# Scores taken ahead in the expert layer: where plain fp32 products stand, and which engine splits the weights for the others

## The chip, the core and the metric

The kernel runs on one core of one Trainium2 chip. The metric is device time in microseconds (us). A core has TensorE (PE in the profile, its weight loads PEld), VectorE (DVE), ScalarE (ACT), GpSimd (POOL), and SyncE (SP), which here only issues transfers. Each engine works through its own list of instructions in a fixed order and waits where an operand isn't ready.

## The reference

Two layers of a diffusion backbone over 512 latent and 256 context tokens of width 1024. Each layer ends in an expert layer (PEER) with 16384 experts, each one row of `exp_u` and one of `exp_v`. A token picks 16 experts for each of 8 heads:

```python
def retrieve(xc):                                     # 128 tokens
    q = (xc @ w_q).reshape(128, 8, 2, 128)
    s = jnp.einsum('thpd,hpnd->thpn', q, sub_keys)    # against 2 x 128 keys a head
    sv, si = lax.top_k(s, 16)
    ...                                               # 16 best sums of pairs
    top_s, top_j = lax.top_k(cand_s, 16)
    e_idx = jnp.take_along_axis(cand_i, top_j, axis=-1)
    gate = jax.nn.softmax(top_s, axis=-1)
    act = gelu(jnp.einsum('thkd,td->thk', exp_u[e_idx], xc))
    return jnp.einsum('thk,thkd->td', gate * act, exp_v[e_idx])
```

## The kernel before

The expert layer (`ffn`, line 1509 on) treats most token tiles of 128 densely: four in layer 0, three in layer 1 (`nd`, so 512 or 384 columns, `ND`). For these it computes the scores of all 16384 experts, as 128 blocks of 128 experts, multiplies them by a sparse matrix of gates, and multiplies the result into `exp_v`. The other tiles (two of the context in layer 0, one in layer 1) gather their rows of the table by indirect transfers on GpSimd.

A score block is made by `score` (line 1538) in one of two forms.

- Plain fp32 (`native`, through `linear`, line 661): one transfer of 512 KB puts the block's weights straight into the tile `wh`, and TensorE multiplies eight slices of them with the fp32 tokens `h[2]`. These stand in tiles that the program calls `row`. The profile shows 16 matmul records per block, `mm<-row,wh`.
- Split (`split`, line 647, and `product`, line 672): the transfer goes to a tile `w`. ScalarE rounds it to `wh` (line 657), a second engine subtracts to get the low part `wl` (line 658), and TensorE makes 24 products with the high and low parts of the tokens, `hhi` and `hlo`: `mm<-hlo,wh`, `mm<-hhi,wh`, and last `mm<-hhi,wl`.

The pool `wts` holds two pairs of `wh` and `wl` in layer 0 and three in layer 1. The tile `w` has three buffers in layer 0 (pool `wload`) and two in layer 1.

After the retrieval (`retrieve`), a stage runs once per layer that is called the spreading stage here. For each tile, `candidates` (line 1441 on) finds the 16 experts of each head, on VectorE with some additions on GpSimd (`ci`, line 1457). For each dense tile `d`, `spread` (line 1746) then builds the gate matrix in 16 rounds, four to each quarter `q`. A round has four comparisons and products on VectorE (`A`, `B`, `H`, `L`, lines 1770 to 1773), 32 small fp16 products on TensorE (`ch<-A,H` and `ch<-A,L`), and two evacuations on ScalarE (`stage`, line 1781). Each quarter ends in a store of 2048 KB (`Wd<-stage`, line 1783). A tile's rounds begin with transposes on TensorE (line 1756) that need VectorE's `af` (line 1753).

The spreading gives TensorE little to do, so 44 of the 128 score blocks (`SK`, the list `early`) are computed inside this stage, ahead of their use, and parked in memory (`gd`). `ahead(n)` (line 1547) brings their number up to `n`, and after each quarter it is asked for a share of the 44 in proportion. In layer 0 all 44 blocks are plain fp32. In layer 1 the even ones are plain and the odd ones split, with GpSimd as the second engine. The other 84 blocks are split with VectorE in the main loop behind the stage. A scheduler fixes the order on each engine from the program; the rounds and the blocks are interleaved there.

Of the kernel before, what the change touches and what calls it, by code (L numbers as in the profile page):

```python
# [156 lines left out]
SK = 44  # L157
# [87 lines left out]
class K:  # L245
# [1263 lines left out]
    def ffn(self, li):  # L1509
# [4 lines left out]
        nc, io = self.nc, self.io  # L1514
        nd = 3 if li else 4
# [6 lines left out]
        gd = self.dram.tile([SK, 128, ND], F32, name=f"gd{li}")  # L1522
        with ExitStack() as es:
# [14 lines left out]
            def score(a, eng, native=False):  # L1538
                if native:
                    p = self.linear(io["uT"][li, a], (None, None, h[2]), ND)  # L1540
                else:
                    p = self.product(self.split(io["uT"][li, a], eng), h, ND)
                g = dp.tile([128, ND], F32, name="g", bufs=4 if li else 3)
                nc.scalar.activation(g, p[:, 0:ND], AF.Gelu)  # L1544
                return g

            def ahead(n):
                while nsk[0] < min(n, SK):
                    nc.sync.dma_start(gd[nsk[0]], score(early[nsk[0]], nc.gpsimd, not li or nsk[0] % 2 == 0))  # L1549
                    nsk[0] += 1  # L1550

            nsk, early = [0], [(2 * n + 1) * 64 // SK for n in range(SK)]
            with ExitStack() as e1:
                tk = P("topk", e=e1)
                sv = tk.tile([128, nt, 16, 16], F32, name="sv")
                si = tk.tile([128, nt, 16, 16], U32, name="si")
                with ExitStack() as e2:
                    hs = []
                    hc = None if li else P("hc", e=e2)
                    for b in ((1,) if li else (1, 0)):  # L1560
                        T = TL if b else TC
                        hb = self.norm_apply(li, 1, b, self.xs if b else self.xc, T, self.rl if b else self.rc, fp if b else hc)
                        if b:
                            h = hb
                        for j, i in enumerate(gathered if b == li else ()):
                            xk = pk.tile([128, 1024], F32, name="xt", tag=("xk", "acc")[j])
                            self.token_major(hb[2], i, xk)
                            nc.sync.dma_start(xd[j], xk)
                        hs.append((hb, T, 2 if b > li else 0))
                    for _ in self.retrieve(li, hs, sv, si, self.wts):  # L1570
                        yield 10
                t2, st = P("cand", 2, e=e1), P("wst", 2, e=e1)
                due = 0.0
                for n, i in enumerate(gathered + dense):
                    self.candidates(sv[:, i], si[:, i], idx[i], gate[i], tk, t2)
                    yield 5
                    if i in gathered:
                        if li:
                            picks.fetch(2)
                        continue  # L1580
                    d = n - len(gathered)
                    for q in self.spread(d, idx[i], gate[i], Wd, tk, st):
                        if q is not None:
                            ahead((SK * (4 * d + q) + 4 * nd - 1) // (4 * nd))
                        elif not li:
                            due += GP
                            picks.fetch(int(due))
                        yield 3
                ahead(SK)
            base, NP = len(picks.rows), picks.n - (0 if li else REST)  # L1590
            cp, ew = P("coef", 2), ExitStack()
            wv = P("wv", 3 if li else 4, e=ew)
# [212 lines left out]
```

## Time and profile before

| what | value |
|---|---|
| three runs | 5423.01, 5433.58 (median), 5465.13 us |
| the profiled execution | 5431.71 us, of it 5429.9 us span |
| granted TensorE clock over the span | 0.932 |
| TensorE, VectorE, ScalarE, GpSimd busy | 91%, 70%, 35%, 22% |
| spreading stage of layer 0, with the blocks ahead | about 1430 to 1850 us |
| spreading stage of layer 1, with the blocks ahead | about 4210 to 4530 us |

Times inside the profile count from the start of the span. A busy share over the whole span mixes many stages, so the two spreading stages are read alone, in windows: which engine is full there, and what the other one waits for. The start of one matmul record to the start of the next tells its price better than its length, since matmuls overlap.

### The profile page before, as it was taken

The page shows a single profiled execution, that of the slowest core. Times are in us where ns is not written, and L with a number is a line of the kernel's source. Part 1 is how long each engine was busy: PE and PEld are TensorE (multiplying, and loading weights), DVE is VectorE, ACT ScalarE, POOL GpSimd, SP SyncE. Part 2 cuts the span into 40 slices and gives each one's busy share as a digit, 9 for nine tenths or more (in the row PEclk, how much of TensorE's full clock was granted, in tenths as well). Part 3 has the DMA queues.
Part 4 walks back from the last instruction along what each step waited for, and adds up shares of the span by engine and source line. Part 5 has one row for each costly group of instructions (what it writes and reads, how often), then busy time and mean ns, then how long its engine had stood idle before and what let it go on. Part 6 is the DMA issues. An engine that isn't in the chain of part 4 may idle for free. (4 is left out here: it accounts for less than half of the span.)

```text
span 5429.9 us, 75527 instructions
## 1 busy us (share of the span) xinstructions
PE 4933.1 (91%) x28525; PEld 3699.6 (68%) x28525; DVE 3819.7 (70%) x8269; ACT 1895.7 (35%) x3396; POOL 1185.2 (22%) x891
## 2 busy tenths in 40 slices
PE   7987999889989999999999779888889889999998
PEld 4765676547644588887878436656657667888887
DVE  6367666656896488888888874666636986777776
ACT  5322222443254333333333212222223454444442
POOL 2322122221200022222222241211122321111110
PEclk9987899899999999999999899777889999999999
DMA  6310121342365788888888773100022668888885
GB/s 203 105 37 20 58 87 48 114 156 66 110 188 162 238 328 317 321 330 320 320 328 318 289 271 112 66 1 1 1 76 84 198 197 300 324 321 310 321 321 206
DMA packets 392490, 1028.15 MB, mean 189 GB/s; under 512 B 31443, under 2 KB 198644, under 8 KB 336572
## 3 DMA queue, kind: packets, MB, share of 16 engines
q1 hardware_dynamic: 336828, 620.64, 34.1%
q0 software_dynamic: 55296, 402.68, 19.7%
q8 instruction: 224, 3.67, 0.3%
q14 instruction: 142, 1.16, 0.1%
HBM read 920.19 MB, written 103.02 MB: 188 GB/s over the span
## 5 line engine op out<-in xcount | busy, mean ns | idle before, releaser
L203 POOL DMA_INDIRECT row<-in_uv,idx x384 | 538.4, 1402 | 1884.4 <-DVE acc L241 1606.7
L657 ACT ACTIVATE wh<-w 128x1024 fp32r<-128x1024 f32 x515 | 545.5, 1060 | 977.9 <-PE mm L272 444.5
L272 PE MATMUL mm<-hlo,wh 128*128 128x512 f32 (+2 forms) x2240 | 804.5, 364 | 17.6 <-DVE hlo L636 6.7
L272 PE MATMUL mm<-hhi,wh 128*128 128x512 f32 (+2 forms) x2240 | 796.6, 360 | 0.0
L658 DVE TENSOR_TENSOR wl<-w,wh 128x1024 fp32r<-128x1024 f32 x424 | 516.0, 1219 | 252.7 <-ACT wh L657 242.2
L241 DVE SCALAR_TENSOR_TENSOR acc<-row,act,acc 128x1024 f32<-128x1024 f32 x381 | 490.3, 1287 | 34.0 <-ACT act L237 33.6
L272 PE MATMUL mm<-hhi,wl 128*128 128x512 f32 (+2 forms) x2240 | 481.5, 356 | 0.0
L219 DVE SCALAR_TENSOR_TENSOR row<-row,xk 128x1024 f32<-128x1024 f32 x384 | 470.6, 1226 | 14.2 <-DMA row<-in_uv,idx 13.9
L272 PEld LDWEIGHTS mm<-hlo,wh 128*128 128x128 f32 x2240 | 427.8, 191 | 77.3 <-DVE hlo L636 9.0
L272 PE MATMUL mm<-row,wh 128*128 128x512 f32 (+1 forms) x1056 | 453.3, 572 | 29.0 <-DMA wh<-in_uT 24.4
L272 PEld LDWEIGHTS mm<-hhi,wh 128*128 128x128 f32 x2240 | 427.9, 191 | 53.0 <-issue 1.4
L272 PEld LDWEIGHTS mm<-hhi,wl 128*128 128x128 f32 x2240 | 392.9, 189 | 44.6 <-issue 1.2
L658 POOL TENSOR_TENSOR wl<-w,wh 128x1024 fp32r<-128x1024 f32 x91 | 227.2, 2500 | 616.9 <-ACT wh L657 368.1
L272 PEld LDWEIGHTS mm<-row,wh 128*128 128x128 f32 x1056 | 194.4, 194 | 208.3 <-issue 159.3
L236 ACT ACTIVATE act<-act 128x1 f32<-128x1 f32 x384 | 76.0, 198 | 523.1 <-DVE row L219 522.9
L1781 ACT ACTIVATE stage<-ch 128x512 f32<-128x512 f32 x224 | 218.2, 1103 | 61.4 <-PE ch L272 59.5
L1544 ACT ACTIVATE g<-mm 128x512 f32<-128x512 f32 (+1 forms) x256 | 137.8, 539 | 230.6 <-PE mm L272 200.1
L272 PE MATMUL rw<-wh,cl 128*128 128x512 f32 x512 | 200.8, 392 | 7.4 <-DVE cl L1612 4.4
L272 PE MATMUL mm<-h,wh 128*128 128x512 f32 (+1 forms) x480 | 194.2, 551 | 11.9 <-DMA hv<-in_hvec 10.7
L272 PE MATMUL rw<-wl,ch 128*128 128x512 f32 x512 | 200.5, 392 | 0.0
L272 PE MATMUL ch<-wh,cl 128*128 128x512 f32 x512 | 199.7, 390 | 0.0
L272 PE MATMUL ch<-wl,ch 128*128 128x512 f32 x512 | 199.4, 390 | 0.0
(541 smaller groups left out, 10390.3 us busy)
## 6 DMA issues: line engine op xcount, KB each, us to landing
w<-in_uv SPq DMA_DIRECT2D x256, 512.0 KB
w<-in_uT SPq DMA_DIRECT2D x190, 512.0 KB
Wd<-stage SPq DMA_DIRECT2D x28, 2048.0 KB
w<-in_mod_w SPq DMA_DIRECT2D x192, 256.0 KB
wh<-in_uT SPq DMA_DIRECT2D x66, 512.0 KB
W<-Wd SPq DMA_DIRECT2D x32, 1024.0 KB
W<-Wd SPq DMA_DIRECT2D x32, 768.0 KB
w<-in_wq SPq DMA_DIRECT2D x32, 512.0 KB
```

The lines of the kernel that those rows point to most:

```text
L203: self.nc.gpsimd.indirect_dma_start(out=row, out_offset=None, in_=self.k.io[f"uv{self.li}"], in_offset=bass.IndirectOffsetOnAxis(ap=self.t ...
L219: nc.vector.scalar_tensor_tensor(row[:, 0:1024], row[:, 0:1024], 1.0, self.x, op0=OP.mult, op1=OP.mult, accum_out=act)
L236: nc.scalar.activation(act, act, AF.Gelu)
L241: nc.vector.scalar_tensor_tensor(self.acc, row[:, 1024:], act, self.acc, op0=OP.mult, op1=OP.add)
L272: self.nc.tensor.matmul(out, lhsT, rhs, start=start, stop=stop, skip_group_check=True)
L657: self.nc.scalar.activation(wh[:, s], w, AF.Copy)
L658: eng.tensor_tensor(wl[:, s], w, wh[:, s].bitcast(F32), op=OP.subtract)
L1544: nc.scalar.activation(g, p[:, 0:ND], AF.Gelu)
L1781: nc.scalar.activation(stage[:, :, u:u + 4].rearrange("p a t -> p t a"), p, AF.Copy, scale=1 / GS)
```

## The change

The plain products move to the front of each stage and the split ones to the back, and VectorE replaces GpSimd in the split. As long as the tile being spread belongs to the first half (`2 * d < nd`), a block is plain fp32; after that it is split, with VectorE as the second engine.

```diff
-            def ahead(n):
+            def ahead(n, native):
                 while nsk[0] < min(n, SK):
-                    nc.sync.dma_start(gd[nsk[0]], score(early[nsk[0]], nc.gpsimd, not li or nsk[0] % 2 == 0))
+                    nc.sync.dma_start(gd[nsk[0]], score(early[nsk[0]], nc.vector, native))
                     nsk[0] += 1
...
-                            ahead((SK * (4 * d + q) + 4 * nd - 1) // (4 * nd))
+                            ahead((SK * (4 * d + q) + 4 * nd - 1) // (4 * nd), 2 * d < nd)
...
-                ahead(SK)
+                ahead(SK, False)
```

With `nd` = 4, the last call for a tile of the first half is at d = 1, q = 3 and asks for ceil(44 x 7 / 16) = 20 blocks. Layer 0 so has 20 plain and 24 split blocks in place of 44 and 0. With `nd` = 3, tiles 0 and 1 count as the first half, the last call there asks for ceil(44 x 7 / 12) = 26, and layer 1 has 26 plain and 18 split blocks in place of 22 and 22.

On TensorE, in layer 0, the first split block stands just ahead of the transposes of the third tile (d = 2). The piece of the difference begins behind the last round of the second tile:

```order
 L272 LDWEIGHTS L
 L272 MATMUL ch<-A,L 128x128
-L272 MATMUL mm<-row,wh 128x512 x15
+L272 MATMUL mm<-row,wh 128x512 x9
+L272 MATMUL mm<-hlo_11440,wh 128x512
+L272 MATMUL mm<-hhi_11439,wh 128x512
+L272 MATMUL mm<-hlo_11440,wh 128x512
+L272 MATMUL mm<-hhi_11439,wh 128x512
```

Nine products of plain blocks are left where fifteen were (in this order a plain block counts eight), and two whole split blocks and the start of a third follow them ahead of the transposes.

On VectorE, in the rounds of layer 0's last tile (d = 3), nothing but the rounds stood before:

```order
L1773 TENSOR_TENSOR L<-B,T_15770 128x1024
L1770 TENSOR_TENSOR A<-iota_92,T_15770 128x1024
L1771 TENSOR_TENSOR B<-iota_92,T_15770 128x1024 x2
L1772 TENSOR_TENSOR H<-B,T_15770 128x1024
L1773 TENSOR_TENSOR L<-B,T_15770 128x1024
L1771 TENSOR_TENSOR B<-iota_92,T_15770 128x1024
L1772 TENSOR_TENSOR H<-B,T_15770 128x1024
```

Now the same place in the changed kernel:

```order
L1773 TENSOR_TENSOR L<-B,T_15990 128x1024
L658 TENSOR_TENSOR wl<-w,wh 128x1024
L1770 TENSOR_TENSOR A<-iota_92,T_15990 128x1024
L1771 TENSOR_TENSOR B<-iota_92,T_15990 128x1024
L658 TENSOR_TENSOR wl<-w,wh 128x1024
L1772 TENSOR_TENSOR H<-B,T_15990 128x1024
L1773 TENSOR_TENSOR L<-B,T_15990 128x1024
```

The 24 subtractions of layer 0 stand like this between comparisons and products of rounds: four ahead of the first round of d = 2, nine between there and the end of the candidates of d = 3, and eleven in or behind the rounds of d = 3. In layer 1 two stand ahead of the rounds of d = 2 and sixteen in or behind them.

On GpSimd, in the candidates of layer 1, the subtractions stood among the gathers of rows (`row<-in_uv,idx`):

```order
L658 TENSOR_TENSOR wl<-w,wh 128x1024
L203 DMA row<-in_uv,idx_33528 128x2048 x2
L658 TENSOR_TENSOR wl<-w,wh 128x1024
L203 DMA row<-in_uv,idx_33528 128x2048 x2
L658 TENSOR_TENSOR wl<-w,wh 128x1024
```

In the changed kernel only the gathers and the additions of the candidates are left there:

```order
L1457 TENSOR_TENSOR ci<-sf 128x8x6
L1457 TENSOR_TENSOR ci<-sf 128x8x8
L203 DMA row<-in_uv,idx_34008 128x2048 x5
L1457 TENSOR_TENSOR ci<-sf 128x8x16
L1457 TENSOR_TENSOR ci<-sf 128x8x8
```

Outside the two stages the order of the instructions is the same in both kernels.

## Rows read from the trace of the kernel before

**Rows 1.** The page, part 1: busy time, share of the span, instructions.
```profile
PE 4933.1 (91%) x28525; PEld 3699.6 (68%) x28525; DVE 3819.7 (70%) x8269; ACT 1895.7 (35%) x3396; POOL 1185.2 (22%) x891
```

**Rows 2.** Windows, layer 0: length; PE, PEld, DVE, ACT, POOL busy; clock, DMA share, GB/s.
```profile
1580.00:1630.00 50.00, 42.26 (x300) 24.66 (x298) 48.24 (x112) 33.54 (x37) 0.00 (x0) 0.98 0.77 223
1633.00:1850.00 217.00, 199.89 (x898) 100.59 (x897) 105.66 (x232) 80.64 (x98) 5.06 (x8) 1.00 0.59 176
```

**Rows 3.** Windows, layer 1, same columns.
```profile
4210.00:4420.00 210.00, 177.00 (x1066) 133.69 (x1064) 201.36 (x553) 103.36 (x130) 61.29 (x47) 0.93 0.64 199
4420.00:4490.00 70.00, 62.53 (x423) 47.17 (x424) 47.09 (x66) 37.88 (x46) 17.42 (x5) 0.98 0.61 187
```

**Rows 4.** Waits of TensorE, 1640 to 1850 us: total, times, longest.
```profile
PE mm L272 <- DMA wh<-in_uT: 11.6, 8, 2.1
PE ch L272 <- ACT stage L1781: 5.0, 16, 0.7
```

**Rows 5.** Waits of TensorE, 4210 to 4540 us.
```profile
PE tr L1756 <- DVE af L1753: 13.2, 3, 5.1
...
PE ch L272 <- DVE L L1773: 4.3, 5, 1.5
PE mm L272 <- DMA wh<-in_uT: 4.0, 2, 2.2
```

**Rows 6.** Timeline of TensorE, layer 0: start, length, instruction, wait before it.
```profile
1728.56 7.11 PE L272 MATMUL mm<-row,wh 128*128 128x512 f32 x16 [1.82 <-DMA wh<-in_uT]
1735.51 0.38 PE L1756 MATMUL tr<-ident,af 128*128 128x128 f32 x2
...
1851.23 0.80 PE L272 MATMUL mm<-hlo,wh 128*128 128x512 f32 x1
1851.86 0.39 PE L272 MATMUL mm<-hhi,wh 128*128 128x512 f32 x1
...
1857.11 0.39 PE L272 MATMUL mm<-hlo,wh 128*128 128x512 f32 x1
```

**Rows 7.** Timeline of TensorE, layer 1: a split block, then a plain one.
```profile
4401.25 0.63 PE L272 MATMUL mm<-hlo,wh 128*128 128x384 f32 x1
...
4405.73 5.32 PE L272 MATMUL mm<-row,wh 128*128 128x384 f32 x16
4410.59 0.63 PE L272 MATMUL mm<-hlo,wh 128*128 128x384 f32 x1
```

**Rows 8.** Groups by form, 4230 to 4560 us: the subtraction on VectorE, on GpSimd.
```profile
L658 DVE TENSOR_TENSOR wl<-w,wh 128x1024 fp32r<-128x1024 f32 x11 | 13.1, 1217 | 11.0 <-ACT wh L657 7.3 <-PE mm L272 3.6
...
L658 POOL TENSOR_TENSOR wl<-w,wh 128x1024 fp32r<-128x1024 f32 x19 | 54.2, 2850 | 183.9 <-ACT wh L657 173.1 <-PE ch L272 10.8
```

**Rows 9.** Waits of VectorE, 1640 to 1850 us.
```profile
DVE H L1772 <- PE ch L272: 52.2, 7, 17.1
DVE A L1770 <- ACT T L1760: 23.6, 1, 23.6
```

**Rows 10.** Timeline of GpSimd and VectorE, layer 1: instructions alone and beside a subtraction.
```profile
4404.66 2.79 POOL L658 TENSOR_TENSOR wl<-w,wh 128x1024 fp32r<-128x1024 f32 x1 [18.50 <-ACT wh L657]
...
4224.22 0.99 DVE L1474 TENSOR_TENSOR e<-e 128x1600 int16<-128x1600 int16 x1
4405.26 3.03 DVE L1474 TENSOR_TENSOR e<-e 128x1600 int16<-128x1600 int16 x1
...
4234.37 2.43 DVE L1457 TENSOR_TENSOR cs<-sv 128x128 f32<-128x128 f32 x1
4414.33 3.04 DVE L1474 TENSOR_TENSOR e<-e 128x1600 int16<-128x1600 int16 x1
```

**Rows 11.** Timeline of SyncE's queue: the issue behind the store of 1791.37 us.
```profile
1791.37 0.52 SPq L1783 DMA_DIRECT2D Wd<-stage  x1
1795.23 2.16 SPq L1549 DMA_DIRECT2D gd<-g  x1
```

**Rows 12.** The costliest groups of the page: the rounding on ScalarE.
```profile
L657 ACT ACTIVATE wh<-w 128x1024 fp32r<-128x1024 f32 x515 | 545.5, 1060 | 977.9 <-PE mm L272 444.5
```

## The prediction

> **What bounds the kernel now.** I read the page first, then windows over the two spreading stages, then the waits of TensorE and VectorE in them, then single blocks on the timeline. The page's first part says that TensorE is busy 91% of the span [rows 1], so a stage is shortened by taking work or waiting off TensorE, unless another engine is full there.
>
> In layer 0, from the third tile on, TensorE is that engine: it is busy 199.89 of 217 us, VectorE 105.66. Just before, up to 1630 us, VectorE is the fuller one with 48.24 of 50 us against 42.26 [rows 2]. VectorE's largest waits there are for TensorE's small products (52.2 us) and for evacuated transposes that TensorE makes late (23.6 us) [rows 9]. TensorE's own largest wait is for the weights of plain blocks, 11.6 us in 8 times [rows 4].
>
> In layer 1 it is the other way round until 4420 us: VectorE is busy 201.36 of 210 us, TensorE 177.00 [rows 3]. TensorE waits 13.2 us for `af` in front of the transposes, and 4.3 us for `L` [rows 5]. From 4420 us on TensorE leads again, with 62.53 of 70 us against 47.09 [rows 3].
>
> **The change part by part, layer 0.** Here 24 plain blocks become split ones, all from the end of the second tile on, where TensorE leads.
>
> TensorE's work: a plain block of 512 columns takes 1735.51 - 1728.56 = 6.95 us. A split block in a steady run takes 23 steps in 1857.11 - 1851.86 = 5.25 us, so 5.25 x 24 / 23 = 5.48 us for 24; with the first record after a change of kind it is 1857.11 - 1851.23 = 5.88 us [rows 6]. The split blocks will be cut up by rounds and pay some of that entry again and again. I take 5.6, nearer the steady value: 24 x (6.95 - 5.6) = 32.4 us less, with 25.7 and 35.3 as ends.
>
> The Trainium skill ("FP8 and Floating Point Precision", section "TensorE Precision Notes") says that true fp32 takes four passes through the array. Three split products against four passes would make a split block 6.95 x 3 / 4 = 5.21 us and the saving 24 x 1.74 = 41.8 us. The steady run of the trace is slower than that, 5.48 us, so the rows decide and the page's figure stays outside my ends.
>
> The waits for weights: a plain block's transfer goes straight into `wh`, of which there are two, so it can't be issued before TensorE has finished two blocks back; behind a 2048 KB store the queue itself is late by another 2.16 us for the next issue [rows 11]. A split block's transfer goes into one of three `w`, which are free as soon as ScalarE and the subtraction have read them. So of the 11.6 us [rows 4] I expect 7 to go, with ends 0 (the queue stays late, and the wait is for `wh` from ScalarE instead) and 11.6.
>
> ScalarE gets 24 roundings of 1.06 us [rows 12], 25.4 us. It is busy 80.64 of 217 us there [rows 2], so they lie beside its idle time. Behind a rounding that waits stand evacuations of the rounds, for which TensorE waits 5.0 us already [rows 4]; that is part of the loss in order below.
>
> VectorE gets 24 subtractions of 1.217 us [rows 8]. Four stand ahead of the first round of the third tile, where VectorE has been the fuller engine [rows 2], so they may push that tile's rounds back by 4 x 1.22 = 4.9 us (ends 0 and 4.9); I count all of it. The other 20 (24.4 us) have 52.2 + 23.6 = 75.8 us of waits to lie in [rows 9]. But they stand between the instructions of rounds, and one that waits for ScalarE or for a free `wl` holds the `H` and `L` behind it, and with them TensorE's small products. With that cover all gone they would cost 24.4 us. I take 5 us.
>
> Sum for layer 0: -32.4 - 7 + 4.9 + 5 = -29.5 us, from -46.9 to +3.6 with all ends on one side.
>
> **Layer 1.** TensorE: a split block of 384 columns takes 4405.73 - 4401.25 = 4.48 us, a plain one 4410.59 - 4405.73 = 4.86 us [rows 7]. Four more blocks are plain: 4 x 0.38 = 1.5 us more.
>
> GpSimd loses 22 subtractions of 2.85 us each [rows 8]. It isn't the bound, but beside one of them a VectorE instruction stands still: the same step took 0.99 us alone and 3.03 us when GpSimd's ran from 4404.66 us [rows 10]. I find twelve such stretched instructions from 4234 to 4415 us, of which rows 10 show the first and the last. At 2.04 us each that is 24.5 us of VectorE's 201.36. What it is worth on the path is capped by what TensorE waits for VectorE: 13.2 + 4.3 = 17.5 us [rows 5]. TensorE also has about 13 more plain blocks in place of split ones before 4420 us, 13 x 0.38 = 5 us, which fills part of these gaps. 17.5 - 5 leaves 12.5; I take 12 us, ends 0 and 17.5.
>
> The Trainium skill ("SBUF — State Buffer", section "Who interferes with whom") says that a VectorE instruction with two SBUF inputs and a GpSimd instruction that reads SBUF shut each other out for a whole instruction. By that a hold could last GpSimd's whole 2.79 us, 33.5 us for twelve; the trace's pair shows 2.04, and the cap is the same. It speaks against the change in one place: the new subtractions have two inputs as well, and can be held by GpSimd's additions for the candidates.
>
> The plain blocks of the back half had 4.0 us of waits for weights [rows 5]: 2 of them go, ends 0 and 4. Two subtractions stand ahead of the third tile's rounds: 2.4 us, ends 0 and 2.4. The other sixteen, 19.5 us, have 70 - 47.09 = 22.9 us of VectorE's idle time [rows 3]: 2 us, ends 0 and 19.5.
>
> Sum for layer 1: 1.5 - 12 - 2 + 2.4 + 2 = -8.1 us, from 1.5 - 17.5 - 4.0 = -20.0 to 1.5 + 2.4 + 19.5 = +23.4.
>
> Both together: -29.5 - 8.1 = -37.6 us on 5431.7 us, the profiled execution, so 5394.1. The median of the three runs is 1.9 us above the profiled one, so I predict 5396 us. What is late next: in layer 0 from the third tile on still TensorE, with VectorE 24 us closer to it; in layer 1 until 4420 us both at once.
>
> **The rivals.** (A) *Everything falls in.* Queues stay in step: TensorE gets the steady 35.3 and all 11.6 us in layer 0, the whole 17.5 and 4.0 us in layer 1, and only the subtractions that stand ahead of rounds and the 1.5 us are paid: -35.3 - 11.6 + 4.9 = -42.0 and 1.5 - 17.5 - 4.0 + 2.4 = -17.6. That gives 5434 - 59.6 = 5374 us. For it speaks that VectorE has three times the idle time that it needs in layer 0 [rows 9]; against it that TensorE would have to run both stages almost without a gap.
>
> (B) *VectorE becomes the bound.* All 42 subtractions end on the path, 42 x 1.217 = 51.1 us, and TensorE's saving is worth nothing, since it now waits for rounds; only the 24.5 us of holds by GpSimd come back. The time is 5434 + 26.6 = 5460 us, slower than before. The place is the rounds of the third and fourth tile. It decides once VectorE's rounds with subtractions take longer than TensorE's rounds with blocks. From 1633 to 1850 us VectorE is busy 105.7 us, with 24 subtractions 135; TensorE's 199.9 us [rows 2] less 32.4 are 167.5. VectorE would have to lose more than 32 us to order. That speaks against it.
>
> (C) *The transfers decide.* SyncE's queue serves stores, scores and weights in one order and is late behind each 2048 KB store [rows 11]; if the weights for split blocks come no earlier than now, TensorE's saving turns into waits, for `w` and `wh` instead of `wh` alone. Layer 0 gains nothing, layer 1 keeps its 8 us: 5425 us. For it speaks that DMA is what TensorE waits for most in layer 0 [rows 4]; against it that the DMA share there is only 0.59 [rows 2] and that the bytes stay the same.
>
> **How the numbers follow.** My forecast gets 0.58, A 0.24, B 0.05, C 0.13. The range goes from 5365 us, below A (with both layers at their lowest ends, -46.9 and -20.0, it would be 5367), to 5430 us, just above C; B lies outside. One per cent, 54 us, is about what a measurement of this kernel can tell from no change. A lies 60 us below the median, beyond it; the lower edge of my own forecast adds 0.03, so faster by over 1% has 0.27. B is within 1% (+0.5%), and only a worse B goes beyond: 0.02. The rest, 0.71, is within 1%.
>
> **What would show it right or wrong.** In the changed kernel's profile: split blocks of layer 0's back half at 5.5 to 5.9 us each where no round cuts in; TensorE's wait for weights after the third tile's start at a few us; the spreading stage of layer 0 with its early blocks some 30 us shorter, that of layer 1 some 8; no VectorE instruction of 3 us in layer 1 where its neighbours take 1. It is wrong if TensorE's waits for `H`, `L` or `stage` grow by more than 10 us in the third and fourth tile (toward B), if it waits for `wh` or `wl` as long as it did for weights (toward C), or if a stage outside these two changes its length by more than a few us.

## The result, and the profile after

| | before | changed |
|---|---|---|
| median of 13 runs each, us | 5437.35 (5411.38 to 5465.13) | 5380.35 (5362.8 to 5401.56) |
| the profiled execution / its span, us | 5431.71 / 5429.9 | 5380.15 / 5378.2 |
| granted clock over the span | 0.932 | 0.935 |

The changed kernel is faster: the ratio is 0.9897, with a 95% interval of 0.9881 to 0.9914, or 57.0 us between the medians. The prediction was 5396 us.

The page's first part of the changed kernel, against [rows 1], tells almost nothing of this: TensorE has 38.5 us less work, and its share is 91% as before.

```profile
PE 4894.6 (91%) x28685; PEld 3719.0 (69%) x28685; DVE 3836.6 (71%) x8311; ACT 1918.1 (36%) x3416; POOL 1118.1 (21%) x869
```

More is to be seen when each stage is cut at marks that both kernels have: the transposes of the first tile (line 1756), those of the third tile, and the first product of the main loop. The stretch up to the third tile is called the *first part* below, the one behind it the *second part*. First the kernel before, in windows; the columns are those of rows 2.

```profile
1506.35:1638.03 131.68, 117.48 (x699) 64.75 (x700) 124.29 (x346) 74.76 (x87) 8.20 (x14) 0.95 0.66 194
1638.03:1866.25 228.22, 207.57 (x940) 108.05 (x938) 110.06 (x220) 87.64 (x107) 6.00 (x9) 1.00 0.61 186
4271.27:4420.36 149.09, 127.27 (x871) 96.27 (x871) 141.55 (x322) 86.70 (x103) 32.72 (x23) 0.95 0.66 197
4420.36:4537.25 116.89, 103.36 (x624) 80.58 (x624) 60.02 (x78) 55.21 (x69) 24.27 (x9) 0.99 0.73 235
```

The same four parts of the changed kernel:

```profile
1512.50:1642.14 129.64, 120.90 (x737) 70.73 (x737) 126.17 (x336) 78.35 (x91) 10.46 (x16) 0.99 0.72 213
1642.14:1831.77 189.63, 171.92 (x1092) 134.39 (x1093) 134.74 (x254) 110.25 (x126) 1.81 (x7) 1.00 0.68 211
4235.31:4367.56 132.25, 124.13 (x778) 78.92 (x779) 124.89 (x324) 78.14 (x94) 9.70 (x15) 0.99 0.75 212
4367.56:4482.59 115.03, 104.50 (x741) 98.74 (x739) 68.52 (x93) 64.99 (x81) 0.94 (x1) 0.99 0.77 251
```

Read them in pairs. Layer 0 gains 2.0 us in the first part and 38.6 in the second, 40.6 together. TensorE's busy time there falls from 117.48 + 207.57 = 325.05 to 292.82, by 32.2, and its time without work from 34.9 to 26.5, by 8.4. Layer 1 gains 16.8 and 1.9 us. There TensorE's busy time falls by 2.0 only; what shrinks is the time without work, from 35.3 to 18.6. The stretch ahead of layer 1's first part (the *opening* below, from the start of the last group of key products, `rw<-key,qT`, to the first tile's transposes) also gets shorter, from 66.2 to 60.0 us.

That makes 65.6 us at the places of the change, while the spans differ by 51.7. The difference comes from stretches where both kernels have the same instructions in the same order; the last group of layer 0's key products ahead of the stage starts at 1429.24 us before and at 1435.23 in the changed kernel, and in the runs below, which change nothing ahead of this point either, anywhere from 1422.17 to 1464.16. The prediction would have taken a few us of this kind as a sign against itself; with such a spread they are none. So the experiments are judged by the length of their parts, beside the time.

The sum of a layer says more than a single part, because the scheduler moves blocks across the marks. Counted by TensorE's records (16 of `mm<-row,wh` or 8 of `mm<-hlo,wh` a block), layer 0 before has 11.2 early blocks in the first part and 23.2 in the second, the changed kernel 12.6 and 21.9. In layer 1 the opening and the two parts have 10.4, 17.5 and 15.7 before, and 9.4, 16.2 and 18 in the changed kernel (the two blocks of the main loop that each second part ends with are left out).

Waits of TensorE in the changed kernel, layer 0's second part (engine, line waited for: total, times, longest). They answer to [rows 4]; behind them stands only one of 1.3 us for `H`.

```profile
PE ch L272 <- ACT stage L1781: 9.5, 26, 0.7
PE tr L1756 <- DVE af L1753: 2.4, 2, 1.5
PE ch L272 <- DVE A L1770: 1.9, 5, 0.5
```

The waits for weights of plain blocks are gone, and waits for `stage` have grown from 5.0 to 9.5 us. In layer 1's first part these and 0.4 us for `H` are all that is left of [rows 5]; the waits for `L` have vanished:

```profile
PE ch L272 <- ACT stage L1781: 5.8, 19, 0.7
PE tr L1756 <- DVE af L1753: 4.8, 2, 3.9
```

A split block that nothing cuts into, on the timeline of TensorE in layer 0's second part, against [rows 6]: 1801.23 - 1795.79 = 5.44 us.

```profile
1795.79 0.39 PE L272 MATMUL mm<-hlo,wh 128*128 128x512 f32 x1
...
1801.23 0.39 PE L272 MATMUL mm<-hlo,wh 128*128 128x512 f32 x1
```

### The profile page after: what moved, and what is told of

It reads as the page before. It is cut to its first block, busy times and chain, and to the rows that moved or that the text cites. A ratio compares the mean times of both kernels' runs of the same rounds, so it can differ in the third digit from the quotient of the medians.

```text
span 5378.2 us, 75892 instructions
## 1 busy us (share of the span) xinstructions
PE 4894.6 (91%) x28685; PEld 3719.0 (69%) x28685; DVE 3836.6 (71%) x8311; ACT 1918.1 (36%) x3416; POOL 1118.1 (21%) x869
## 5 line engine op out<-in xcount | busy, mean ns | idle before, releaser
L272 PE MATMUL mm<-hlo,wh 128*128 128x512 f32 (+2 forms) x2400 | 863.9, 364 | 16.4 <-DVE acc L1635 6.8
L272 PE MATMUL mm<-hhi,wh 128*128 128x512 f32 (+2 forms) x2400 | 859.9, 362 | 0.0
L658 DVE TENSOR_TENSOR wl<-w,wh 128x1024 fp32r<-128x1024 f32 x466 | 568.4, 1223 | 295.5 <-ACT wh L657 272.7
L272 PE MATMUL mm<-hhi,wl 128*128 128x512 f32 (+2 forms) x2400 | 523.6, 359 | 0.0
L272 PEld LDWEIGHTS mm<-hhi,wl 128*128 128x128 f32 x2400 | 421.9, 188 | 51.7 <-issue 1.9
L272 PE MATMUL mm<-row,wh 128*128 128x384 f32 (+1 forms) x736 | 296.6, 546 | 6.7 <-ACT g L1544 4.4
L658 POOL TENSOR_TENSOR wl<-w,wh 128x1024 fp32r<-128x1024 f32 x69 | 165.8, 2408 | 424.5 <-PE mm L272 226.0
L272 PEld LDWEIGHTS mm<-row,wh 128*128 128x128 f32 x736 | 134.0, 193 | 113.8 <-issue 67.2
L272 PE MATMUL rw<-wh,ch 128*128 128x512 f32 x512 | 200.4, 391 | 0.0
L272 PE MATMUL ch<-wh,ch 128*128 128x512 f32 x512 | 200.0, 391 | 0.0
```

Of the source, the lines that this page charges most:

```text
L272: self.nc.tensor.matmul(out, lhsT, rhs, start=start, stop=stop, skip_group_check=True)
L658: eng.tensor_tensor(wl[:, s], w, wh[:, s].bitcast(F32), op=OP.subtract)
```

## The experiments

Parts are given as first + second part. For orientation: before 131.7 + 228.2 in layer 0 and 149.1 + 116.9 in layer 1; changed 129.6 + 189.6 and 132.2 + 115.0. All ratios are to the kernel before. How far such lengths can be trusted is seen where runs share a layer's program: the sum of its two parts then lies between 319.3 and 319.9 us in layer 0 as changed (five runs), 358.4 and 359.9 as before (three), 247.1 and 249.0 in layer 1 as changed (five), and 265.1 and 267.6 as before (three).

### The two layers apart

The changed kernel with layer 1 as before:

```diff
-score(early[nsk[0]], nc.vector, native)
+score(early[nsk[0]], nc.gpsimd if li else nc.vector, nsk[0] % 2 == 0 if li else native)
```

> Layer 0 as in the changed kernel (20 plain blocks, then 24 split by VectorE), layer 1 as before (plain and split in turns, GpSimd). Theory: the two layers' gains are independent and add up. From the first transposes of the third tile to the first product of the main loop, layer 0 takes 228.2 us before and 189.6 us after the change; here 190 +-3. Layer 1 from its first tile's transposes to the main loop takes 266.0 before and 247.3 after; here 266 +-3. In all some 36 to 41 us less than before (-0.7%). Rival: the gain of layer 1 is a consequence of layer 0's (rows gathered earlier, a different clock); then layer 1 is shortened here as well and the time is close to the changed kernel's.

Measured: 5406.26 us, ratio 0.9942 (0.9918 to 0.9965). Layer 0 has 130.7 + 188.8, layer 1 148.2 + 119.4.

And the changed kernel with layer 0 as before:

```diff
-score(early[nsk[0]], nc.vector, native)
+score(early[nsk[0]], nc.vector, native if li else True)
```

> Layer 0 as before (44 plain blocks), layer 1 as in the changed kernel (26 plain, then 18 split by VectorE). Theory: layer 0's back part takes 228 +-3 us, layer 1's stage 247 +-3, in all 16 to 21 us less than before (-0.35%). Rival (layer 1's gain hangs on layer 0's): layer 1's stage stays at 266.

Measured: 5419.74 us, ratio 0.9962 (0.9944 to 0.9981); 132.0 + 227.5 and 132.8 + 116.3, with an opening of 60.7 us in layer 1. The parts of both are as expected; the first run's whole gain, 33.2 us, is a little below the 36 to 41 expected. The gains, 0.58% and 0.38%, add up to 0.96%, beside 1.03% for the whole change, so the layers can be studied one at a time.

### Layer 0: how much is the late weights?

The kernel before, where plain blocks of layer 0 put their weights into `wh` and the idle `wl` by turns, four buffers in place of two:

```diff
-                    p = self.linear(io["uT"][li, a], (None, None, h[2]), ND)
+                    p = self.ps("mm")
+                    w = self.wts.tile([128, 8, 128], F32, name="wl" if not li and nsk[0] % 2 else "wh")
+                    nc.sync.dma_start(w, io["uT"][li, a])
+                    for k in range(8):
+                        self.mm(p[:, :ND], w[:, k], h[2][k][:, :ND], k == 0, k == 7)
```

> The kernel before, all of layer 0's early blocks plain fp32, but their weights go by turns into the buffers of wh and of wl (which stand idle there), so four blocks can be under way in place of two. It takes the waits for weights alone out of the gain: TensorE waited 6.8 us for them between the first and the third tile's transposes of layer 0 and 11.6 us behind (18.4 us). Theory (most of layer 0's 40.6 us is products saved, 24 blocks at about 1.35 to 1.5 us): those waits fall under 4 us, the stage from the first transposes to the main loop takes 342 to 352 us (359.9 before, 319.3 after the change), in all 8 to 18 us less than before. Rival (the late weights were the whole cost of a plain block): it takes 320 to 328 us.

Measured: 5422.21 us, ratio 0.9964 (0.9938 to 0.9991); layer 0 has 127.8 + 211.9 = 339.6 us, a little shorter than expected. The two largest waits of TensorE from 1500 to 1850 us in this kernel (its `stage` and `af` are lines 1785 and 1757):

```profile
PE ch L272 <- ACT stage L1785: 10.9, 33, 0.7
PE tr L1760 <- DVE af L1757: 10.5, 3, 9.2
```

Four more follow, of 1.9 us and less, and no wait for weights is among them. So 20.3 of the 40.6 us can be had without splitting a single block, from weights that come in time; and in the other 20.3 us the products' 32.2 us have partly been given back.

### Layer 0: what the subtractions cost

The changed kernel without the subtraction in layer 0's 24 split blocks (the rounded part is used a third time, so TensorE's work is the same):

```diff
-            eng.tensor_tensor(wl[:, s], w, wh[:, s].bitcast(F32), op=OP.subtract)
-        return wh, wl
+            if not self.bare:
+                eng.tensor_tensor(wl[:, s], w, wh[:, s].bitcast(F32), op=OP.subtract)
+        return wh, wh if self.bare else wl
...
+                    self.bare = not li
                     nc.sync.dma_start(gd[nsk[0]], score(early[nsk[0]], nc.vector, native))
+                    self.bare = False
```

> The changed kernel, with one edit: the 24 split blocks taken ahead in layer 0 leave the subtraction out and use the rounded part a third time (the low part of these weights is left out of the result). Layer 1 as in the changed kernel (132.2 and 115.0 us). Doing each subtraction twice cost 16.6 us for 29 us of work. Theory: the first 29 us cost something too, since VectorE's spare time in the rounds is used up in places: 3 to 12 us less over both parts, of it up to 4.9 in the first. Rival: the first 24 are hidden whole and only what goes beyond the cover is paid, so 317 to 321 us for both parts, as in the changed kernel (319.3).

Measured: 5388.74 us, ratio 0.9895 (0.9844 to 0.9946); layer 0 has 127.6 + 187.4 = 315.0 us. The time can't tell this from the changed kernel; the parts are 2.0 and 2.2 us shorter, 4.2 in all. Only the sum tells what the subtractions cost, because the first part holds about half a split block less here (37 products of split blocks in place of 50). TensorE's largest wait in the second part, for `stage`, is nearly what it was: 8.1 us in 23 times.

And with each of these subtractions done twice:

```diff
-            eng.tensor_tensor(wl[:, s], w, wh[:, s].bitcast(F32), op=OP.subtract)
+            for _ in range(1 + self.twice):
+                eng.tensor_tensor(wl[:, s], w, wh[:, s].bitcast(F32), op=OP.subtract)
```

> The changed kernel, but in layer 0 each of the 24 early subtractions is done twice on VectorE (the same values again), 24 x 1.22 = 29 us more of VectorE's work in the back part. It measures the cover. Theory (the subtractions lie beside waits of VectorE): back part 190 to 197 us, 0 to 7 more than the 189.6 of the changed kernel. Rival (VectorE is the next bound and each subtraction is on the path): 205 to 219 us.

Measured: 5404.59 us, ratio 0.993 (0.9905 to 0.9954); 136.3 + 199.6 = 335.9 us, 16.6 more than the changed kernel. The second part lies between what the two theories gave for it; the first, for which they gave nothing, is 6.7 us longer and holds almost a block more (73 products of split blocks against 50). Taken with the run ahead of it: the first 24 x 1.22 = 29 us of VectorE's work cost 4.2 us, the second 29 us cost 16.6. The cover is real and nearly used up.

The same 24 blocks split by GpSimd:

```diff
-score(early[nsk[0]], nc.vector, native)
+score(early[nsk[0]], nc.vector if li else nc.gpsimd, native)
```

> The changed kernel, but layer 0's 24 split blocks are split by GpSimd. Theory: TensorE's work is that of the changed kernel, and each subtraction on GpSimd holds VectorE by some 2 us, 24 x 2 = 49 us beside about 55 us of VectorE's idle time: the back part of layer 0 takes 193 to 205 us (228.2 before, 189.6 after), the front 130 +-3. Rival (it is the products alone, the second engine doesn't matter where TensorE leads): 188 to 192 us.

Measured: 5390.73 us, ratio 0.9901 (0.9866 to 0.9937); 133.3 + 201.6 = 334.9 us, 15.6 longer than with VectorE, and the second part is where the theory expected it. Windows of its two parts, then of the kernel without the subtraction:

```profile
1516.95:1650.25 133.30, 118.09 (x724) 68.36 (x724) 129.76 (x335) 78.45 (x91) 19.31 (x19) 0.97 0.72 213
1650.25:1851.87 201.62, 177.19 (x1106) 139.95 (x1106) 130.47 (x232) 111.35 (x127) 63.59 (x28) 0.97 0.64 196
```

```profile
1522.68:1650.31 127.63, 119.16 (x724) 68.74 (x724) 123.18 (x335) 78.21 (x91) 11.00 (x16) 0.98 0.71 207
1650.31:1837.73 187.42, 173.75 (x1105) 137.60 (x1106) 111.07 (x232) 108.12 (x127) 4.12 (x7) 1.00 0.71 220
```

The third figure behind the comma is VectorE. Both kernels give it the same 567 instructions (335 + 232) and no subtraction, and yet it is busy 129.76 + 130.47 = 260.2 us in the one and 123.18 + 111.07 = 234.3 in the other. 24 subtractions on GpSimd cost VectorE 26 us; in the changed kernel, which does them itself, it is busy 126.17 + 134.74 = 260.9 us. With GpSimd as the second engine, fourteen of VectorE's instructions run 1.2 to 2.5 us past the shortest of their form, 27.1 us in all. Handing this work to GpSimd saved VectorE nothing. What makes the kernel slower is that the rounds come later: over both parts TensorE waits 12.1 us for `H` in place of 2.8, 15.4 for `af` in place of 11.7, and 2.2 for `L`, for which it waited nowhere. It has no wait for `wl` itself.

### Layer 1: the engine, the place, or both?

Order of plain and split as changed, GpSimd as the second engine again in layer 1:

```diff
-score(early[nsk[0]], nc.vector, native)
+score(early[nsk[0]], nc.gpsimd if li else nc.vector, native)
```

> The changed kernel, but layer 1's 18 split blocks are split by GpSimd; plain blocks still stand in front. It tells the place from the engine. Theory (GpSimd's subtraction holds VectorE, which hurts only where VectorE is full): the front of layer 1, from the first tile's transposes to the third's, keeps its gain (149.1 us before, 132.3 after; here 132 +-3), since no subtraction stands there on either engine; the back part (116.9 before, 115.0 after) gets 0 to 12 us longer through holds and the later wl. Rival (the engine is all): the front goes back to 149. Second rival (the place is all): the back part stays at 115 too and the kernel is as fast as the changed one.

Measured: 5397.1 us, ratio 0.9915 (0.9891 to 0.9939); layer 1 has 133.8 + 125.2, both where the theory expected them. Then the other half of the change, VectorE as the second engine, with plain and split in turns as before:

```diff
-score(early[nsk[0]], nc.vector, native)
+score(early[nsk[0]], nc.vector, nsk[0] % 2 == 0 if li else native)
```

> The changed kernel, but in layer 1 plain and split blocks take turns as before, with VectorE as the second engine. Theory: some 13 subtractions of 1.22 us, 16 us, come into the front of layer 1 where VectorE is full, and the holds by GpSimd, 24.5 us, are gone; TensorE's limits leave the front at 140 to 148 us (149.1 before, 132.3 after), and the back part at 112 to 117. Rival (the holds alone decide, a subtraction on VectorE is hidden): the front takes 132 to 135 us.

Measured: 5383.28 us, ratio 0.9894 (0.9869 to 0.9919); layer 1 has 147.6 + 110.5 = 258.0 us, with an opening of 63.0. Its short second part holds 15 early blocks, the changed kernel's 18. The place (plain blocks in front) is what shortens the first part; the engine shortens the second, by 10.2 us against the run with GpSimd. Neither half of the edit gives both. As times these two and the changed kernel can't be told apart: their intervals overlap.

What GpSimd's subtractions cost was then measured alone: the kernel before, where the 22 split blocks of layer 1 leave the subtraction out, as above with `self.bare = bool(li)`.

> The kernel before, with one edit: the 22 split blocks taken ahead in layer 1 leave the subtraction out and use the rounded part a third time, so TensorE makes the same 24 products a block and neither GpSimd nor VectorE subtracts for them (the low part of these weights is left out of the result). Layer 0 as before (131.7 and 228.2 us). Theory: GpSimd's subtractions cost layer 1 its time by holding VectorE beside the candidates, so without them the opening falls from 66.2 to 60 us and the first part from 149.1 to 132 us (+-3), as in the changed kernel. Rival: what brought the first part down was that its blocks are all plain (no split block's chain of transfer, rounding and subtraction between rounds); then the first part stays at 144 us or more here, as it did with VectorE in GpSimd's place (147.6).

Measured: 5426.36 us, ratio 0.9971 (0.9948 to 0.9993); opening 61.2 us, parts 138.1 + 119.7. Five of the opening's 6.2 us and 11.0 of the first part's 16.8 come from GpSimd's subtractions. It is the holds and not a late `wl`: the kernel before has no wait of TensorE for `wl` in this stretch, while its waits for `af` and `L` in the first part fall from 12.7 to 2.1 us without the subtractions. The second part takes about what it does in the runs with layer 1 as before (116.9 to 119.4). The remaining 5.8 us of the first part, which neither theory had, come with the order: the changed kernel has one block less there than this run (16.2 against 17.2), and no wait for weights where this run has one of 4.3 us.

The holds can be seen in one row each. First the kernel before from the opening to the end of the first part (4205 to 4420 us), the 32 instructions of line 1474 with their shortest, median and longest time in ns, then the changed kernel (4175 to 4368 us):

```profile
L1474 DVE TENSOR_TENSOR e<-e x32: 248/451/3035, 4224.2 to 4418.4; 128x1600 int16<-128x1600 int16 x8, 128x768 int16<-128x768 int16 x8, 128x384 int16<-128x384 int16 x8, 128x192 int16<-128x192 int16 x8
```

```profile
L1474 DVE TENSOR_TENSOR e<-e x32: 251/453/993, 4194.4 to 4363.9; 128x1600 int16<-128x1600 int16 x8, 128x768 int16<-128x768 int16 x8, 128x384 int16<-128x384 int16 x8, 128x192 int16<-128x192 int16 x8
```

Counted over VectorE's timeline, thirteen instructions of the kernel before run 2.0 to 2.6 us past the shortest of their own form there, 28.4 us in all (the prediction's twelve, from 4234 us on, make 26.3); in the changed kernel, and in the one without GpSimd's work, none does. All thirteen end 0.05 to 0.85 us behind the end of a subtraction on GpSimd, each by less than the time it takes alone. In [rows 10] GpSimd's ends at 4404.66 + 2.79 = 4407.45 us and VectorE's at 4405.26 + 3.03 = 4408.29, 0.84 us later, where it takes 0.99 alone: VectorE stands still until GpSimd's subtraction has ended.

### Can it be had better?

The changed kernel with plain and split in turns in layer 1's second part alone:

```diff
-score(early[nsk[0]], nc.vector, native)
+score(early[nsk[0]], nc.vector, native or (li and nsk[0] % 2 == 0))
```

> The changed kernel with one edit: in layer 1 the second part (from the third tile on) takes plain and split blocks in turns, the first part stays plain. Layer 0 is as in the changed kernel (129.6 and 189.6 us). Theory: the gain of layer 1's first part comes from its plain blocks without any subtraction beside the candidates, so it stays at 132 us (+-3); the second part does better with fewer subtractions, as with turns throughout, 110 to 112 us against 115.0. The stage 243 us (+-3) against 247.3, the whole time some 4 us less than the changed kernel, which the clock of whole runs can hardly tell. Rival: the short second part of the kernel with turns throughout was paid for by its long first part (blocks that had been done earlier); then the second part is 115 us or more here.

Measured: 5387.36 us, ratio 0.9895 (0.9868 to 0.9921); layer 1 has 132.3 + 121.9, and the expected 110 to 112 is missed by ten. The rival holds: the short second part of the run with turns throughout was paid for in its first part. Here it holds 18 early blocks again. TensorE is busy 114.41 us in it against 104.50 in the changed kernel, and the price of a block says why. First two plain blocks of this run with a split one between them, then the starts of two split blocks in a row in the changed kernel:

```profile
4450.87 5.32 PE L272 MATMUL mm<-row,wh 128*128 128x384 f32 x16
...
4460.19 5.32 PE L272 MATMUL mm<-row,wh 128*128 128x384 f32 x16
```

```profile
4451.40 0.33 PE L272 MATMUL mm<-hlo,wh 128*128 128x384 f32 x1
...
4455.56 0.34 PE L272 MATMUL mm<-hlo,wh 128*128 128x384 f32 x1
```

A plain and a split block in turns take 4460.19 - 4450.87 = 9.32 us, two split ones in a row 2 x (4455.56 - 4451.40) = 8.32. Nine pairs with 1.00 us more each make 9.0 of the 9.9 us. The two steps of [rows 7], 4.48 + 4.86 = 9.34 us, are the same pair; cut at the change of kind, they make the split block look too dear and the plain one too cheap. The plain block costs about 1.0 us more, not 0.38.

The same with four buffers for layer 0's plain blocks, as above:

> The kernel with turns behind in layer 1, and in layer 0 the plain blocks put their weights into wh and wl by turns, so four buffers in place of two. Theory: the plain blocks of layer 0's first part hardly wait for weights any more in the changed kernel (0.3 us in the first part), so the four buffers bring 0 to 2 us there: 128 to 130 us for the first part, 188 to 191 for the second; layer 1 as in the kernel with turns behind. Rival: the buffers are worth as much as they were to the kernel before, 4 us of the first part and more in the second: 125 and 180 us.

Measured: 5381.27 us, ratio 0.9884 (0.9855 to 0.9914); layer 0 has 129.8 + 188.5, layer 1 132.3 + 120.7. Late weights were worth 20.3 us to the kernel before and 1.0 us, hardly more than the spread, to the changed one: once its first part is plain and its second split, they come in time. This run also tells what the split itself is worth in layer 0: with four buffers in both, plain blocks alone take 339.6 us, and with the split ones behind it is 318.3, 21.3 less. Last, no plain blocks at all, all 44 split by VectorE in both layers:

```diff
-score(early[nsk[0]], nc.vector, native)
+score(early[nsk[0]], nc.vector, False)
```

> The changed kernel with no plain blocks at all: all 44 early blocks of both layers are split by VectorE. Theory (plain blocks are worth their longer products only where VectorE is full): 20 subtractions, 24 us, come into layer 0's front and lengthen it from 129.6 to 142 to 154 us, though TensorE has 20 x 1.5 = 30 us less to do in the stage; layer 1's front goes from 132.3 to 150 to 162 us; the back parts stay within 5 us of 189.6 and 115.0. In all 25 to 50 us slower than the changed kernel. Rival (TensorE's work decides everywhere): the stages are shorter than the changed kernel's, layer 0's by up to 30 us.

Measured: 5451.83 us, ratio 1.0023 (0.9997 to 1.005); 160.2 + 176.9 and 160.1 + 104.6, and openings 14.3 and 18.1 us longer than in the changed kernel. In the parts and the openings that is 67.7 us more than the changed kernel, far over the 25 to 50 expected. The first parts are 30.6 and 27.9 us longer, the second ones 12.7 and 10.5 shorter. The two parts of layer 0:

```profile
1527.88:1688.10 160.22, 126.90 (x810) 97.68 (x811) 136.57 (x348) 89.95 (x100) 8.33 (x14) 0.81 0.56 168
1688.10:1865.04 176.94, 153.60 (x978) 119.45 (x977) 129.59 (x249) 101.89 (x117) 5.18 (x7) 0.93 0.65 199
```

TensorE is busy a smaller share than in the changed kernel, waits more often (27.0 us in 59 times for `stage` alone, against 15.4 in 42), and is granted a clock of 0.81 and 0.93 in place of 0.99 and 1.00. In the first part its time without work is 33.3 us in place of 8.7, which is 24.6 of the 30.6 us. How much of the 67.7 us is the clock and how much the waits was not separated.

## Why the prediction was right, and where its steps were off

The time, 5380.35 us, is 16 below the 5396 predicted and well inside the range; faster by 1.03%, it lies at the bound that the text drew between "same" and "faster". The mechanism held in both layers. The sums did not: 29.5 us were forecast for layer 0 and 40.6 came out; for layer 1 it was 8.1 against 24.9 with the opening. That the time is only 16 us off is partly luck: 8.6 of the 65.6 us gained in the stages don't show in the medians, and no run ties that to the change. But rival A ("everything falls in", 5374 us) is nearer: it had 42.0 us for layer 0 and 17.6 for layer 1. Term by term:

- **Products of layer 0**: predicted -32.4, measured -32.2 in TensorE's busy time. The 5.6 us taken per split block was right, with 5.44 for one that nothing cuts into. That it fits to 0.2 us is chance: with four buffers, where the granted clock of the first part is 0.98 in place of 0.95, all-plain blocks keep TensorE busy 322.1 us in place of 325.05, and the saving against that is 29.3. By the four passes that the Trainium skill ("FP8 and Floating Point Precision", section "TensorE Precision Notes") states for true fp32, the prediction's estimate was 41.8 us; by these runs a plain block takes 6.95 / 5.44 = 1.28 times a split one, not 4/3.
- **Waits for weights, layer 0**: predicted -7 of 11.6. This is the term that failed. TensorE's waits for `wh` fall by 18.1 us over both parts, from 18.4 to 0.3. The text looked from 1640 us on and so missed a single wait of 6.56 us at 1631.09 us in the kernel before, and it distrusted the queue, which was not what made them late: with four buffers on the same queue they vanish too.
- **Four subtractions ahead of the third tile's rounds, the other 20, and the order**: predicted +4.9 and +5. Leaving all 24 out brings 4.2 us; the two terms can't be told apart. Against the waits for weights that went (18.1) stands a fall of TensorE's idle time by only 8.4, so other waits grew by 9.7: over both parts those for `stage` from 10.8 to 15.4, for `af` from 9.4 to 11.7, for `A` from none to 1.9, for `H` from 1.9 to 2.8. The subtractions account for 4.2 of it at most, and not for the waits for `stage`, which without them are 8.1 us in the second part in place of 9.5. That ScalarE's 24 roundings stand ahead of the evacuations fits this row; it was not tried apart.
- **GpSimd's holds, layer 1**: predicted -12, capped at 17.5. Without its subtractions the opening and the first part get 5.0 + 11.0 = 16.0 us shorter, so the size was short by 4. The cap was not a cap: the waits of [rows 5] run to 4540 us, and ahead of 4420 those for `af` and `L` make 9.3 + 3.4 = 12.7 us. The first part's 11.0 stay below that; the opening's 5.0 come on top, from a stretch where VectorE is busy 63.4 of 66.2 us and TensorE's largest wait is one that [rows 5] don't show, 7.3 us for `g` (line 1544). The Trainium skill ("SBUF — State Buffer", section "Who interferes with whom") says that a VectorE instruction with two SBUF inputs and a GpSimd instruction that reads SBUF shut each other out for a whole instruction, which the prediction put at 33.5 us for twelve holds as long as all of GpSimd's instruction. The count on VectorE is 26.3 us. The trace agrees with the page even so: VectorE's instructions wait for the rest of GpSimd's, to its end. The place where that rule spoke against the change is hardly there any more: in layer 0's second part GpSimd is busy 1.81 us, and the subtractions (24, and six of the main loop) keep their time, 1.216 to 1.227 us each.
- **What was not in the sum at all, layer 1**: the opening, which the text's windows held but its cap left out, and 5.8 us that the plain blocks in front bring beside the holds, with one block less in the first part. The granted clock of the first part rises from 0.95 to 0.99, and is 0.96 without GpSimd's work; this goes with that gain, but wasn't varied by itself.
- **Plain blocks in place of split ones filling TensorE's gaps** (-5 of the cap): TensorE's busy time in the first part does not grow; it falls from 127.27 to 124.13, with 16.2 blocks in place of 17.5 and a higher granted clock. This term and the +1.5 for four more plain blocks rest on 0.38 us a block, where the runs show about 1.0: by that the four cost 4 us.
- **Subtractions in layer 1** (+2.4 and +2) **and waits for weights there** (-2): the second part is 1.9 us shorter in all, with TensorE busy 1.1 longer and two early blocks more (18 against 15.7). The single terms can't be told apart.

Rival B fell: in layer 0's second part VectorE is busy 134.74 of 189.63 us, TensorE 171.92. The prediction had 135 for VectorE. It put VectorE 24 us closer to TensorE, but TensorE's own work fell too: between their busy times there lay 97.5 us before and 37.2 now, 60 closer. And the run with doubled subtractions shows how near B was: with VectorE busy 155.20 of 199.57 us in the second part, layer 0 already takes 16.6 us longer. Rival C fell with the waits for weights.

## What to carry to other kernels

Fill each stretch with the form of work that spares the engine that is full there: plain products (dear on TensorE, free for VectorE) beside candidates and early rounds, split products (cheaper on TensorE) where VectorE has slack; either half of this edit alone left some 11 us of layer 1's 18.7 behind. Price each form in a run of its own kind, not at a change of kind. Where an engine waits often for a transfer, try more buffers before anything else is rebuilt: here an idle tile gave half of layer 0's gain. And read a helper engine's cost on its neighbour: what counts is the neighbour's busy time for the same instructions with and without the helper's.

## What the runs showed of the hardware

24 subtractions of 128x1024 on GpSimd lengthened VectorE's own 567 instructions by 26.0 us, as much as doing them there (26.7 us more busy time, by 260.9 against 234.3). An instruction of line 1474 that takes 0.99 us alone took 3.03 beside a subtraction on GpSimd in layer 1 before, and ended 0.84 us behind that subtraction's end. A plain and a split block of 384 columns in turns took 9.32 us, two split ones in a row 8.32. And where all blocks were split, the granted clock of layer 0's first part was 0.81 in place of 0.99, with TensorE busy 126.90 of 160.22 us instead of 120.90 of 129.64.
